# Attention queries projected between the second and third column group of the delta net's inputs, in both mixers

## The chip, the cores and the metric

The kernel runs on one core of a Trainium2 chip. The core has a matrix engine (PE), a vector engine (DVE), an activation engine (ACT), a general engine (POOL) and a queue that issues most transfers (SP). They run side by side, each takes its own instructions in a fixed order, and a semaphore holds an instruction until what it needs is done. The metric is device time of one execution in microseconds (us). The kernel before takes 3166.99 us (median of three runs, 3161.59 to 3169.63).

## The reference, cut to what matters

Two blocks follow each other on 256 tokens of width 1024, in float32. The first has two layers, and each layer begins with a mixer that feeds the same normalised input `h` to two branches: a differential attention (`da`) and a gated delta net (`dn`).

```python
proj = h @ w_in[l]
da_q, da_k, da_v, dn_q, dn_k, dn_v, dn_z, dn_b, dn_a, gates = jnp.split(proj, split_points, axis=-1)
y_a = diff_attention(da_q, da_k, da_v, ...)            # rms norm, rope, two softmaxes, difference
y_b = gated_deltanet(dn_q, dn_k, dn_v, dn_z, dn_b, dn_a, ...)
merged = g_a * (y_a @ w_branch_a[l]) + g_b * (y_b @ w_branch_b[l])
x = x + gt1 * (merged @ w_out[l])
h = rms_norm(x, norm2_g[l]) * (1.0 + sc2) + sh2
x = x + gt2 * (jnp.square(jax.nn.relu(h @ w_mlp1[l])) @ w_mlp2[l])
```

In `gated_deltanet`, q, k and v (512 columns each, columns 1536 to 3071 of `w_in`) pass a depthwise convolution over five tokens and a silu. Then q and k are normalised, and chunks of 64 tokens are put through a triangular solve, a scan in each direction, and a gated output norm. `da_q` is columns 0 to 511 of `w_in`, `da_k` and `da_v` the next two times 512. The second block (a sparse attention or a state space mixer, and a retrieval of experts) is computed by code that the change does not touch.

## The kernel before, in words

**Weights.** All large weights are loaded as tiles of 128x1024 floats in the order of one list, the plan, which `weights()` writes. A tile comes by a transfer into one of four raw buffers (`w_raw_t`). Then ACT rounds it to a reduced format (`w_hi`, line 238) and DVE subtracts to get the rest (`w_lo`, line 239). The pair goes into one of three pair buffers, so `w_hi` of a tile waits until PE is through with the tile three places earlier. The code asks for a pair two places ahead. Each product is taken as three matmuls (lines 318, 319, 320: high by high, high by low, low by high).

**Two forms of projection.** `proj_feat` puts out features on the partitions: 256 columns of weights are two tiles and 48 matmuls of 256 columns, and the result fills one PSUM bank. `proj_tok` puts out tokens on the partitions: 512 columns of weights are four tiles and 48 matmuls of 512 columns into two banks, one for each 128 tokens. PSUM banks come from three rings: psA has two banks, psB three, psC three.

**Start of a mixer (here called stage A).** The delta net's q, k and v are six column groups of 256, called cb0 to cb5. `dn(0)` is cb0 and cb1 (q), `dn(1)` is cb2 and cb3 (k), `dn(2)` is cb4 and cb5 (v). cb1 and cb3 go to psB, the others to psA. Each ends in `conv5`: ACT takes the middle tap (line 887), DVE adds four taps for each of two halves (line 891, eight instructions in all, which read the PSUM bank), ACT takes a tanh (893), DVE multiplies (894), PE transposes (line 324), ACT writes out (900). Then a small projection gives the delta net's gates (`exr`, lines 1430 and 1434: its result is copied by DVE, transposed by PE, and copied to `ba`).

**The woven part.** From there on, Python generators are interleaved by `weave`: decay and preparation of the delta net, the triangular solves (line 1249 is one of their matmuls), the scans (1321, 1328), the attention, and `project()`, which puts the remaining projections between them as work that PE can do while chains run on other engines. `project()` goes through `dn(2)`, then `tok` of da_q, da_k and da_v, then gates, z, gates. The attention's preparation of da_q and da_k squares on ACT (949), sums on DVE (950), normalises (957), and rotates with two halves on POOL (959, 960) and two instructions on DVE (961, 962). POOL also writes the masks `TT` of the solves (1208, 1209). Behind the weave `out` ends the delta net (lines 1358 to 1380), with the attention's branch projection (`ya`) beside it, and then follows the branch of the delta net (`yb`).

**What sets the order.** The program is written in this order, and the tile framework then sorts each engine's instructions with a simulated timeline of its own, so that one engine's order differs from the text within a stretch. Queues are in order on the chip.

Of the kernel before, what the change touches and what calls it, by code (L numbers as in the profile page):

```python
# [77 lines left out]
def weights(first=True):  # L78


    out, phase = [], 0

    def add(n, l, r0, c0, a, lane=None):
        out.append((phase, lane or f"m{phase}", n, l, r0, c0, a, 1024 // a))

    def tok(n, l, c0, rows=1024):
        for r0 in range(0, rows, 256):
            add(n, l, r0, c0, 2)

    def tok2(n, l, c0, lane=None):  # L90
        for r0 in (0, 512):
            add(n, l, r0, c0, 4, lane)

    def feat(n, l, c0, lane=None):
        for c in (c0, c0 + 128):
            add(n, l, 0, c, 8, lane)

    def mem_kv(l):
        feat("w_mem_kv_2", l, 0, "pm")
        tok2("w_mem_kv_2", l, 256, "pm")  # L100

    for l in range(2):
        for c0 in range(1536, 3072, 256):
            feat("w_in", l, c0)
        for c0 in (0, 512, 1024):
            tok("w_in", l, c0)
        for c0 in range(4624, 5648, 256):
            feat("w_in", l, c0)
        tok("w_in", l, 3072)
        for c0 in range(3600, 4624, 256):  # L110
            feat("w_in", l, c0)
        for j in (2, 3, 4) if l == 0 else (4,):
            for c0 in (1024 * j, 1024 * j + 512):
                for r0 in range(0, 1024, 256):
                    add("ada_w", l, r0, c0, 2, "plain")
        for n in ("w_branch_a", "w_branch_b"):
            for c0 in (0, 512):
                tok(n, l, c0, 512)
        for c0 in (0, 512):
            tok("w_out", l, c0)  # L120
        for g in range(17):
            if g < 16:
                feat("w_mlp1", l, 256 * g)
            if g == 9 and first:
                mem_kv(l)
            if g:
                for r0 in (256 * g - 256, 256 * g - 128):
                    add("w_mlp2", l, r0, 0, 1)
    if not first:
        out.clear()  # L130
        for l in range(2):
            mem_kv(l)
    for l in range(2):
        phase += 1
        if l == 0:
            n = "a_w_in_2"
            for c0 in (1024, 1280):
                feat(n, 0, c0)
            tok2(n, 0, 768)
            for c0 in (0, 256, 512, 1608):  # L140
                feat(n, 0, c0)
        else:
            n = "b_w_in_2"
            for c0 in (1536, 1792, 2060, 768, 1024, 1280):
                feat(n, 0, c0)
            tok(n, 0, 0)
            tok2(n, 0, 512)
        for c0 in (0, 512):
            tok("w_o_2", l, c0)
        for c0 in range(0, 2048, 256):  # L150
            feat("peer_w_q_2", l, c0)
        for i in range(128 + LAG):
            if i < 128:
                add("peer_u_2", l, 128 * i, 0, 1, f"u{l}" if i >= RAW else f"pu{l}")
            if i >= LAG:
                add("peer_v_2", l, 128 * (i - LAG), 0, 1, f"v{l}")
    return out
# [129 lines left out]
class K:  # L287
# [479 lines left out]
    def mixer1(self, c, Ls, l):  # L767
# [9 lines left out]
        done = set()  # L777
# [31 lines left out]
        def project():  # L809
            yield from dn(2)  # L810
            done.add("v")
            for i, n in enumerate(("daq", "dak", "dav")):
                yield from tok(dat[i])
                done.add(n)
                yield
# [8 lines left out]
            for _ in self.ada(L, (2, 3, 4) if l == 0 else (4,), self.st.plain):  # L824
                yield

        for i in range(2):
            for _ in dn(i):
                pass
        if l == 0:  # L830
            nc.sync.dma_start(self.ct, a["cst"][:, N1:N2])
        ba = sm.tile([128, 2, 16], F32, name="ba")
# [1434 lines left out]
```

## Time and profile before

| what | value |
|---|---|
| median of three runs | 3166.99 us |
| the profiled execution | 3168.19 us |
| its span in the trace | 3166.4 us |
| mean granted clock of PE | 0.96 |
| mixer of layer 0 in the trace | about 38 to 404 us |
| mixer of layer 1 in the trace | about 596 to 955 us |

The span is 1.8 us shorter than the execution's own time. PE is the engine with the most busy time (95%); its clock is either full or half, and 0.96 is a mean over both. In a timeline row the bracket gives how long the engine was idle just before the row and what it waited for. In a row of waits the three numbers are total time, times and the longest. In a row by form or line the last part is idle time before the group.

### The profile page before, as it was taken

Reading aid. Unit: us, or ns where it says so; the run is one execution under the profiler, and the core shown is the slowest. Engines: PE = TensorE matmul, PEld = TensorE weight load, DVE = VectorE, ACT = ScalarE, POOL = GpSimd, SP = SyncE. Lnnn points to the kernel's source line nnn. Section 1 sums busy time; section 2 is a strip of 40 time slices with the busy share of each in tenths; the row PEclk is TensorE's granted clock in tenths of the full one; section 3 lists DMA queues with packets and bytes.
Section 4 is the critical chain, followed back from the end, with each engine's and each line's share of the span. In section 5 each row is a group of like instructions: output and inputs, shape, how many; then the busy total and the mean of one; then the engine's idle time right before and its main releaser. Section 6 shows DMA issues by size and latency. Waiting matters only on the chain.

```text
span 3166.4 us, 54565 instructions
## 1 busy us (share of the span) xinstructions
PE 2994.7 (95%) x21010; PEld 2685.5 (85%) x21010; DVE 2464.6 (78%) x5317; ACT 1553.7 (49%) x2630; POOL 116.0 (4%) x95
## 2 busy tenths in 40 slices
PE   7999899899989999899999999997799999999998
PEld 6798799878869987888999999986588999999987
DVE  7888767886766568698878878777879887887877
ACT  5644455464545546425555455455433545554544
POOL 0211000011100001000000000000100000000000
PEclk9999899999989996899999999998799999999999
DMA  7425578533356651435555555453144555555544
GB/s 255 134 96 179 199 256 300 180 113 120 114 173 209 199 187 34 136 126 161 180 176 178 180 179 176 159 187 119 56 146 141 170 176 180 179 175 179 180 160 147
DMA packets 158201, 522.02 MB, mean 165 GB/s; under 512 B 17320, under 2 KB 24404, under 8 KB 157812
## 3 DMA queue, kind: packets, MB, share of 16 engines
q1 hardware_dynamic: 149408, 502.94, 47.9%
q10 hardware_dynamic: 7348, 11.39, 1.1%
q8 instruction: 165, 2.70, 0.4%
q0 software_dynamic: 1184, 4.19, 0.3%
q14 instruction: 96, 0.79, 0.1%
HBM read 514.23 MB, written 6.59 MB: 164 GB/s over the span
## 4 chain that ended last, share of the span: by engine, by line
PE 77%; DVE 13%; ACT 3%; DMA 3%; issue 2%; POOL 1%; SPq 0%; ACTq 0%; DVEq 0%; POOLq 0%
PE psA L318 14%; PE psA L320 13%; PE psA L319 13%; PE psB L318 8%; PE psB L320 8%; PE psB L319 8%; DVE w_lo L239 3%; PE psA L2013 2%; PE psB L2072 2%; PE psB L324 1%; ACT w_hi L238 1%; PE psB L1257 1%; DMA w_raw_t<-in_peer_u_dram 1%; PE psC L630 1%; PE psB L1249 1%
## 5 line engine op out<-in xcount | busy, mean ns | idle before, releaser
L238 ACT ACTIVATE w_hi<-w_raw_t 128x1024 fp32r<-128x1024 f32 x806 | 850.3, 1057 | 746.5 <-PE psB L319 372.7
L239 DVE TENSOR_TENSOR w_lo<-w_raw_t,w_hi 128x1024 fp32r<-128x1024 f32 x806 | 991.8, 1231 | 241.1 <-ACT w_hi L238 217.2
L318 PE MATMUL psB<-H,w_hi 128*128 128x256 f32 x2128 | 601.2, 283 | 2.8 <-ACT w_hi L238 2.8
L320 PE MATMUL psB<-H,w_lo 128*128 128x256 f32 x2128 | 601.3, 283 | 0.0
L319 PE MATMUL psB<-H,w_hi 128*128 128x256 f32 x2128 | 600.3, 282 | 0.0
L318 PEld LDWEIGHTS psB<-H,w_hi 128*128 128x128 f32 x2128 | 403.8, 190 | 12.2 <-ACT w_hi L238 3.4
L320 PEld LDWEIGHTS psB<-H,w_lo 128*128 128x128 f32 x2128 | 411.1, 193 | 0.6 <-DVE w_lo L239 0.3
L319 PEld LDWEIGHTS psB<-H,w_hi 128*128 128x128 f32 x2128 | 403.6, 190 | 8.4
L318 PE MATMUL psA<-w_hi,Wh 128*128 128x512 f32 x1024 | 390.8, 408 | 0.0
L319 PE MATMUL psA<-w_lo,Wh 128*128 128x512 f32 x1024 | 371.5, 389 | 0.0
L320 PE MATMUL psA<-w_hi,Wl 128*128 128x512 f32 x1024 | 370.4, 392 | 0.0
L318 PE MATMUL psA<-H,w_hi 128*128 128x256 f32 x1056 | 304.0, 289 | 13.0 <-DVE exy L1789 8.0
L320 PE MATMUL psA<-H,w_lo 128*128 128x256 f32 x1056 | 303.5, 288 | 2.8 <-DVE w_lo L239 2.6
L319 PE MATMUL psA<-H,w_hi 128*128 128x256 f32 x1056 | 301.9, 286 | 0.0
L2055 DVE TENSOR_TENSOR oj<-iop,pickj 128x1024 f16<-128x1024 f16 x256 | 176.4, 690 | 111.5 <-PE psB L2072 111.0
L327 ACT ACTIVATE Wh<-W 128x256 fp32r<-128x256 f32 x256 | 106.7, 419 | 316.4 <-issue 251.6
L320 PEld LDWEIGHTS psA<-w_hi,Wl 128*128 128x128 f32 x1024 | 191.8, 188 | 43.8
L319 PEld LDWEIGHTS psA<-w_lo,Wh 128*128 128x128 f32 x1024 | 193.1, 189 | 35.8 <-DVE w_lo L239 0.2
L318 PEld LDWEIGHTS psA<-w_hi,Wh 128*128 128x128 f32 x1024 | 192.3, 188 | 33.2
L318 PEld LDWEIGHTS psA<-H,w_hi 128*128 128x128 f32 x1056 | 204.3, 194 | 17.7 <-issue 10.7
L320 PEld LDWEIGHTS psA<-H,w_lo 128*128 128x128 f32 x1056 | 205.1, 194 | 4.8 <-DVE w_lo L239 4.0
L319 PEld LDWEIGHTS psA<-H,w_hi 128*128 128x128 f32 x1056 | 204.5, 194 | 1.0 <-issue 0.7
(593 smaller groups left out, 5012.1 us busy)
## 6 DMA issues: line engine op xcount, KB each, us to landing
w_raw_t<-in_wst_dram SPq DMA_DIRECT2D x368, 512.0 KB, 3.9
w_raw_t<-in_peer_u_dram SPq DMA_DIRECT2D x256, 512.0 KB, 3.3
w_raw_t<-in_peer_v_dram SPq DMA_DIRECT2D x256, 512.0 KB, 3.3
aw<-in_ada_w_dram SPq DMA_DIRECT2D x24, 1024.0 KB, 7.5
bd<-bd ACTq DMA_DIRECT2D x1, 2304.0 KB
H<-in_ada_w_dram SPq DMA_DIRECT2D x2, 1024.0 KB
gd<-ga ACTq DMA_DIRECT2D x4, 512.0 KB, 9.8
qkT<-gd ACTq DMA_DIRECT2D x4, 512.0 KB, 5.4
```

What stands on the lines that cost most here:

```text
L238: nc.scalar.activation(out=hi, in_=raw, func=AF.Copy)
L239: nc.vector.tensor_tensor(out=lo, in0=raw, in1=hi.bitcast(F32), op=OP.subtract)
L318: mm(ps, lhsT=lh, rhs=rh, start=first, stop=False)
L319: mm(ps, lhsT=lh, rhs=rl, start=False, stop=False)
L320: mm(ps, lhsT=ll, rhs=rh, start=False, stop=last)
L324: self.nc.tensor.transpose(out, in_, self.ident[:p, :p])
L327: self.nc.scalar.activation(out=hi, in_=src, func=AF.Copy, scale=scale)
L630: mm(ps[:, k:k + 1], lhsT=acc[:, k * 128:(k + 1) * 128], rhs=self.ones[:, 0:1], start=(i == 0), stop=(i == len(accs) - 1))
L1249: nc.tensor.matmul(px[:, hc(d, h)], lhsT=NT[d, t][:, hs(h)], rhs=cls(TI[d, t][:, hs(h)], s, 1 - d), start=True, stop=True)
L2013: nc.tensor.matmul(ps[:, 0:256], lhsT=w[:, k * 128:k * 128 + 128], rhs=whole[:, k, :], start=(k == 0), stop=(k == 7))
L2055: v.tensor_tensor(out=oj, in0=self.iop.unsqueeze(1).to_broadcast([128, H, 128, 2]), in1=two(pick[1][:, tb], 128), op=OP.is_equal)
L2072: nc.tensor.matmul(ps[:, 64 * k:64 * k + 64], lhsT=oj[:, x, :, y], rhs=oi[:, x, :, :, y].rearrange("p n i -> p (n i)"), start=True, stop=True)
```

## The change

The plan puts the tiles of `w_in` columns 0 to 511 (da_q, four tiles) behind the first two column groups of the delta net. Before, they stood behind all six. The code follows: after `dn(0)` it runs `tok(dat[0])` and then `dn(1)`, all in front of the weave, marks `daq` as done, and `project()` goes on from `dn(2)` with da_k. The instructions are the same in number and shape on every engine, apart from a few waits and register instructions. Line numbers grow by 3 from line 106 on and by 4 from about line 827 on.

```diff
--- before.py
+++ after.py
@@ -100,9 +100,12 @@
         tok2("w_mem_kv_2", l, 256, "pm")
 
     for l in range(2):
-        for c0 in range(1536, 3072, 256):
+        for c0 in (1536, 1792):
             feat("w_in", l, c0)
-        for c0 in (0, 512, 1024):
+        tok("w_in", l, 0)
+        for c0 in range(2048, 3072, 256):
+            feat("w_in", l, c0)
+        for c0 in (512, 1024):
             tok("w_in", l, c0)
         for c0 in range(4624, 5648, 256):
             feat("w_in", l, c0)
@@ -809,7 +812,7 @@
         def project():
             yield from dn(2)
             done.add("v")
-            for i, n in enumerate(("daq", "dak", "dav")):
+            for i, n in ((1, "dak"), (2, "dav")):
                 yield from tok(dat[i])
                 done.add(n)
                 yield
@@ -824,9 +827,10 @@
             for _ in self.ada(L, (2, 3, 4) if l == 0 else (4,), self.st.plain):
                 yield
 
-        for i in range(2):
-            for _ in dn(i):
+        for g in (dn(0), tok(dat[0]), dn(1)):
+            for _ in g:
                 pass
+        done.add("daq")
         if l == 0:
             nc.sync.dma_start(self.ct, a["cst"][:, N1:N2])
         ba = sm.tile([128, 2, 16], F32, name="ba")
```

Three places show how the orders differ. The names carry the buffer's number: `psA_529` is one allocation of a psA bank, `w_hi_476` and `w_lo_477` are one pair.

PE, mixer 0, behind the last matmuls of cb1 (psB_443). Before, cb2 stands there (psA_529):

```order
L318 MATMUL psB_443<-H0_241,w_hi_446 128x256
L319 MATMUL psB_443<-H1_242,w_hi_446 128x256
L320 MATMUL psB_443<-H0_241,w_lo_447 128x256
L318 MATMUL psA_529<-H0_241,w_hi_476 128x256
L319 MATMUL psA_529<-H1_242,w_hi_476 128x256
L320 MATMUL psA_529<-H0_241,w_lo_477 128x256
```

After, the da_q projection stands there. These are its rows at the step from the first 128 tokens (psA_529) to the second (psA_530, the bank that cb0's psA_345 had):

```order
L323 MATMUL psA_529<-w_hi_551,H1_242 128x512
L321 MATMUL psA_529<-w_hi_551,H0_241 128x512
L322 MATMUL psA_529<-w_lo_552,H0_241 128x512
L323 MATMUL psA_529<-w_hi_551,H1_242 128x512
L321 MATMUL psA_530<-w_hi_476,H0_241 128x512
L322 MATMUL psA_530<-w_lo_477,H0_241 128x512
L323 MATMUL psA_530<-w_hi_476,H1_242 128x512
L321 MATMUL psA_530<-w_hi_476,H0_241 128x512
```

Forty-eight matmuls of 512 columns have moved to this place, and the second bank of them is that of cb0.

DVE, at the same place: the convolution of cb0 (`exy_418`) and cb1 (`exy_504`). Before, these are the rows about the last instruction that reads cb0's bank:

```order
L239 TENSOR_TENSOR w_lo_649<-w_raw_t_530,w_hi_648 128x1024
L891 SCALAR_TENSOR_TENSOR exy_418<-psA_345,vec_93,exy_418 128x255
L891 SCALAR_TENSOR_TENSOR exy_590<-psA_529,vec_93,exy_590 128x254
L891 SCALAR_TENSOR_TENSOR exy_504<-psB_443,vec_93,exy_504 128x254
L891 SCALAR_TENSOR_TENSOR exy_418<-psA_345,vec_93,exy_418 128x254
L891 SCALAR_TENSOR_TENSOR exy_590<-psA_529,vec_93,exy_590 128x255
```

After, they are the rows from the third pair of da_q (`w_lo_552`) to that instruction:

```order
L242 TENSOR_TENSOR w_lo_552<-w_raw_t_444,w_hi_551 128x1024
L895 SCALAR_TENSOR_TENSOR exy_418<-psA_345,vec_93,exy_418 128x254
L895 SCALAR_TENSOR_TENSOR exy_504<-psB_443,vec_93,exy_504 128x254
L895 SCALAR_TENSOR_TENSOR exy_504<-psB_443,vec_93,exy_504 128x255
L895 SCALAR_TENSOR_TENSOR exy_418<-psA_345,vec_93,exy_418 128x254
L895 SCALAR_TENSOR_TENSOR exy_504<-psB_443,vec_93,exy_504 128x255
L895 SCALAR_TENSOR_TENSOR exy_418<-psA_345,vec_93,exy_418 128x255
L895 SCALAR_TENSOR_TENSOR exy_504<-psB_443,vec_93,exy_504 128x254
L895 SCALAR_TENSOR_TENSOR exy_418<-psA_345,vec_93,exy_418 128x255
L895 SCALAR_TENSOR_TENSOR exy_418<-psA_345,vec_93,exy_418 128x254
```

No convolution of a third group (`exy_590` before) stands among them any more, and nine convolution instructions are left between that pair and the release of cb0's bank.

DVE, mixer 0, about the last convolution instruction of cb2, whose bank cb5 takes next. Before, cb2 is psA_529 with `exy_590`, and `w_lo_1229` is the first pair of da_q, three places behind the second pair of cb4:

```order
L891 SCALAR_TENSOR_TENSOR exy_676<-psB_615,vec_93,exy_676 128x254
L891 SCALAR_TENSOR_TENSOR exy_590<-psA_529,vec_93,exy_590 128x255
L239 TENSOR_TENSOR w_lo_1229<-w_raw_t_915,w_hi_1228 128x1024
L891 SCALAR_TENSOR_TENSOR exy_1047<-psA_914,vec_93,exy_1047 128x254
L891 SCALAR_TENSOR_TENSOR exy_590<-psA_529,vec_93,exy_590 128x254
L891 SCALAR_TENSOR_TENSOR exy_676<-psB_615,vec_93,exy_676 128x254
```

After, cb2 is psA_605 with `exy_666`, cb4 is psA_1025, and `w_lo_1364` is the first pair of da_k, again three places behind cb4's second pair (`w_hi_1028`):

```order
L956 TENSOR_SCALAR ss_998<-ss_998 128x16
L895 SCALAR_TENSOR_TENSOR exy_666<-psA_605,vec_93,exy_666 128x255
L242 TENSOR_TENSOR w_lo_1364<-w_raw_t_1026,w_hi_1363 128x1024
L895 SCALAR_TENSOR_TENSOR exy_1170<-psA_1025,vec_93,exy_1170 128x254
L895 SCALAR_TENSOR_TENSOR exy_752<-psB_691,vec_93,exy_752 128x254
L341 TENSOR_SCALAR rs_i_1006<-ss_998 128x16
L895 SCALAR_TENSOR_TENSOR exy_666<-psA_605,vec_93,exy_666 128x254
```

The pair has kept its place in front of that last instruction, and small instructions of the da_q preparation (lines 956, 341) have come between.

PE, mixer 1, the end of `out`. Before, the last of its matmuls (line 1363) is followed by 43 matmuls of the attention's branch (`ya`):

```order
L1363 MATMUL psB_8802<-N11_7456,AT11_6776 64x128
L320 MATMUL psA_8979<-ya0_8191,w_lo_8910 128x256
L318 MATMUL psA_8979<-ya0_8191,w_hi_8969 128x256
L319 MATMUL psA_8979<-ya1_8192,w_hi_8969 128x256
L320 MATMUL psA_8979<-ya0_8191,w_lo_8970 128x256
L318 MATMUL psA_8979<-ya0_8191,w_hi_8969 128x256
```

After (line 1367), the transposes of `out` follow at once, and behind them the delta net's branch (`yb`):

```order
L1367 MATMUL psB_8802<-N11_7591,AT11_6899 64x128
L327 MATMUL psB_8859<-base_58,D1_8764 128x128 x4
L327 MATMUL psB_8894<-base_58,D1_8764 128x128 x4
L321 MATMUL psA_9053<-yb0_8829,w_hi_8975 128x256
L321 MATMUL psA_9084<-yb0_8829,w_hi_8975 128x256
L322 MATMUL psA_9053<-yb1_8830,w_hi_8975 128x256
L323 MATMUL psA_9053<-yb0_8829,w_lo_8976 128x256
```

The branch matmuls have moved ahead, in among the scan.

On POOL the rotation halves and the masks are in a new order. Before, in both mixers: masks `TT00`, `TT10`, `TT01`, then four halves of da_q, then `TT11`, then four of da_k. After, in mixer 1: two halves of da_q stand behind `TT00`, the other two between the two steps of `TT01`, two of da_k in front of `TT11`, and the last two between the two steps of `TT11`. In mixer 0 the first two of da_k stand between the two steps of `TT11` and the last two behind it.

## Rows read from the trace of the kernel before

**Rows 1.** The page, part 1: busy time by engine.

```profile
PE 2994.7 (95%) x21010; PEld 2685.5 (85%) x21010; DVE 2464.6 (78%) x5317; ACT 1553.7 (49%) x2630; POOL 116.0 (4%) x95
```

**Rows 2.** Timeline, PE, mixer 0, column groups 5 and 6 (start us, us, engine line operation).

```profile
69.64 0.28 PE L320 MATMUL psA<-H,w_lo 128*128 128x256 f32 x1
71.64 0.63 PE L324 MATMUL psC<-base,exy 128*128 128x128 f32 x4 [1.72 <-DVE exy L894]
74.33 0.35 PE L318 MATMUL psA<-H,w_hi 128*128 128x256 f32 x1 [2.07 <-DVE exy L891]
74.53 0.28 PE L319 MATMUL psA<-H,w_hi 128*128 128x256 f32 x1
74.64 0.28 PE L320 MATMUL psA<-H,w_lo 128*128 128x256 f32 x1
```

**Rows 3.** Windows of mixer 0 behind that wait (length, busy time and count by engine, clock).

```profile
75.20:78.60 3.40, 3.40 (x18) 3.40 (x17) 3.12 (x8) 1.08 (x2) 0.00 (x0) 0.50 0.27 105
78.60:82.00 3.40, 3.40 (x32) 3.40 (x31) 2.86 (x5) 3.15 (x13) 0.00 (x0) 1.00 0.00 0
```

**Rows 4.** Timeline, DVE, the same stretch.

```profile
72.19 1.21 DVE L239 TENSOR_TENSOR w_lo<-w_raw_t,w_hi 128x1024 fp32r<-128x1024 f32 x1
73.33 0.86 DVE L891 SCALAR_TENSOR_TENSOR exy<-psA,vec,exy 128x254 f32<-128x254 f32 x2
74.11 0.47 DVE L891 SCALAR_TENSOR_TENSOR exy<-psB,vec,exy 128x254 f32<-128x254 f32 x1
```

**Rows 5.** ACT by form, 36 to 92 us (count, busy, mean ns, idle before).

```profile
L238 ACT ACTIVATE w_hi<-w_raw_t 128x1024 fp32r<-128x1024 f32 x14 | 14.9, 1065 | 12.3 <-PE psA L319 8.1 <-ACT exy L887 1.6 <-issue 1.3
```

**Rows 6.** Timeline, PE, two matmuls of 512 columns.

```profile
99.34 0.39 PE L318 MATMUL psA<-w_hi,H 128*128 128x512 f32 x1
99.57 0.39 PE L319 MATMUL psA<-w_lo,H 128*128 128x512 f32 x1
```

**Rows 7.** Waits of PE in mixer 0, 36 to 340 us (total, times, longest).

```profile
PE psB L324 <- DVE ext L1430: 2.0, 1, 2.0
PE psC L324 <- DVE exy L894: 1.7, 1, 1.7
PE psC L324 <- DVE oo L1018: 1.1, 1, 1.1
```

**Rows 8.** Waits of PE in mixer 1, 596 to 960 us.

```profile
PE psB L324 <- DVE D L1380: 4.8, 1, 4.8
PE psC L324 <- DVE D L962: 2.7, 1, 2.7
PE psA L318 <- DVE exy L891: 2.1, 1, 2.1
PE psC L324 <- DVE exy L894: 1.5, 1, 1.5
```

**Rows 9.** Windows of mixer 0 (start:end, length, busy time and count by engine, clock).

```profile
36.00:92.00 56.00, 49.35 (x358) 46.03 (x359) 48.95 (x108) 33.15 (x76) 0.00 (x0) 0.97 0.49 160
168.00:257.00 89.00, 88.79 (x722) 83.66 (x721) 74.12 (x179) 44.97 (x98) 7.27 (x7) 1.00 0.38 126
257.00:298.00 41.00, 37.54 (x278) 34.60 (x277) 31.81 (x79) 16.40 (x42) 7.98 (x7) 0.88 0.34 110
```

**Rows 10.** Windows of mixer 1 about the wait for L962.

```profile
727.10:737.40 10.30, 10.30 (x49) 10.30 (x50) 4.88 (x7) 1.35 (x3) 0.00 (x0) 0.50 0.16 52
737.40:745.00 7.60, 7.60 (x55) 6.08 (x54) 2.16 (x7) 2.77 (x7) 0.00 (x0) 1.00 0.00 0
```

**Rows 11.** Lines by form, 640 to 730 us: POOL's rope.

```profile
L960 POOL TENSOR_TENSOR exr<-D,ropes 128x256 f32<-128x256 f32 x4 | 5.8, 1449 | 0.0
L959 POOL TENSOR_TENSOR exr<-D,ropes 128x256 f32<-128x256 f32 x4 | 3.7, 924 | 4.1 <-DVE exy L894 2.4 <-DVE D L962 1.8
```

**Rows 12.** Windows of mixer 1, the end of the delta net.

```profile
878.30:883.50 5.20, 5.20 (x45) 5.19 (x45) 4.45 (x18) 1.23 (x2) 0.00 (x0) 1.00 0.01 2
883.50:888.90 5.40, 0.58 (x6) 0.35 (x5) 4.97 (x14) 1.89 (x3) 0.00 (x0) 0.88 0.38 107
```

## The prediction

> **What bounds the kernel now.** I began with the page's busy times: PE is busy for 95% of the span and DVE for 78% [rows 1]. So the order of PE's work can gain only where PE waits, or where its clock is low. The list of PE's waits in the two mixers came next, since the change moves nothing outside them: it shows a few waits of 1 to 5 us, nearly all of them for DVE [rows 7, 8]. The windows tell where PE is the bound. In the solves of mixer 0 PE is busy for 88.79 of 89.00 us. In stage A it is busy for 49.35 of 56.00 with DVE at 48.95, so the two share that stage. Behind the last solve it is busy for 37.54 of 41.00, at a mean clock of 0.88 [rows 9]. Last came timelines and windows about the waits of stage A [rows 2 to 4].
>
> In stage A, cb4's last matmul starts at 69.64 and cb5's first at 74.33. Between them stand waits of 1.72 and 2.07 us with four transposes [rows 2]. Behind DVE's `w_lo`, which starts at 72.19, come three convolution instructions, and the second one at 73.33 frees cb5's bank [rows 4]. That pair is three places behind cb4's second pair, so its `w_hi` could not start before PE had done with cb4. The wait thus belongs to the ring of three pairs more than to DVE's load.
>
> **The change part by part.** The counts of instructions stay as they are, so the sum of this change is what PE's idle time and low clock become. One projection is 48 matmuls at 0.23 us, 99.34 to 99.57 [rows 6], so 11.0 us of PE work comes into stage A and leaves later stages. Counted in the two orders, it leaves as follows. Mixer 0: 2.1 us before the first solve, 6.1 in the solves, 2.8 behind them. Mixer 1: nothing before the first solve, 3.4 in the solves, 1.8 from there through the scan, 5.9 from the first of `out`'s matmuls on. A matmul of 256 columns counts 0.11 us there, 74.53 to 74.64 [rows 2]. Where the work leaves a stretch in which PE never waits, the stretch gets that much shorter and the move costs nothing. Six points remain.
>
> *The new bank step.* The second bank of da_q is cb0's, and DVE must finish cb0's convolution first. From cb1's last matmul on: `w_hi_551` takes 1.06 us [rows 5], since its buffer is the one of cb1's second pair. Its `w_lo` takes 1.14 from start to start, and nine convolution instructions take 0.39 each (two in 0.78, 73.33 to 74.11) [rows 4]. That is 1.06 + 1.14 + 9 x 0.39 = 5.7 us, against 18 x 0.23 = 4.1 us of matmuls into the first bank. The new wait is 1.6 us, up to 2.0 with the semaphores; I take 1.8 in each mixer, 3.6 in both. If DVE has a backlog there it is more, and if ACT prepares early, less: 0 to 3.
>
> *The old bank step (cb4 to cb5).* The chain stays: w_hi 1.06, w_lo 1.14, then three convolution instructions and a small one, 1.4, together 3.6 us. The two waits before are 1.72 + 2.07 = 3.8 us in mixer 0 [rows 2], and 2.1 + 1.5 = 3.6 in mixer 1 [rows 8]. I count nothing. If DVE stands 0.5 us behind, it is +0.5; if the extra 11 us had let DVE catch up, the wait would go (first rival).
>
> *The clock.* After the wait of 2.07 us the granted clock is 0.50 for 3.4 us, the lower level, and then 1.00 again [rows 3]. That costs half of it, 1.7 us. A new wait may bring such a stretch. I count none, and 1.7 us in each mixer at the high end.
>
> The Trainium skill, page "TensorE: Matmul & The Clock Gate", section "A second HAM failure mode: psum-queue depth-cycling", says that short idle times between groups of matmuls that cycle through PSUM banks can make the clock swing between its two levels, and that the loss is in throughput. The rows agree that it can follow such a wait. By that rule the sum below would be 3.4 us higher.
>
> *The rope and the masks.* In mixer 1 PE waits 2.70 us for da_q's or da_k's rotation (962) [rows 8], and the clock then stays at 0.50 for 10.30 us [rows 10], which costs half of it, 5.15 us. Together that is 7.85. With da_q ready some 50 us earlier, half of POOL's rotations stand earlier, and DVE has lost the da_q preparation there. But two rotation halves now stand between the steps of the last mask, 0.92 + 1.45 = 2.4 us of POOL [rows 11], and the last solve's start waits for it. The ends are -7.9 and +2.4. I take -3.9: the wait shrinks but part of the low clock stays.
>
> *Behind the solves in mixer 0.* 2.8 us of cover leaves a stretch where PE already waits on chains (1.1 for `oo`) [rows 7], and where it is idle for 3.5 of 41 us [rows 9]. Ends 0 and +2.8; I take the middle, +1.4.
>
> *`out` in mixer 1.* Before, 43 branch matmuls fill 878.3 to 883.5, and then PE waits 4.8 us for the chain through DVE's 1380 [rows 8, 12]. DVE is busy for 4.45 of those 5.20 us and for 4.97 of the next 5.40 [rows 12], so the chain is DVE's. With the branch matmuls gone ahead, the chain stays and PE idles for 10 us instead of 4.8. So 5.2 us of the moved work saves nothing. DVE has up to two fewer branch instructions in the way, some 0.8 us. I take +4.4; ends +2 (DVE's chain was longer for the branch) and +6 (the clock stays low for longer).
>
> The sum: 3.6 + 0 + 0 - 3.9 + 1.4 + 4.4 = +5.5 us. On the profiled execution of 3168.19 us (span 3166.4 and 1.8 around it) that is 3173.7. The median stands 1.2 below that execution, so I forecast 3172.5.
>
> **The rivals.**
>
> *The inserted work is cover.* Between cb1 and cb2 DVE gets 11 us in which PE has other work, and could clear all its convolutions. Then both waits of stage A vanish: 3.8 us and 1.7 of low clock in mixer 0, 3.6 and 1.7 in mixer 1, 10.8 in all. With the rope's -7.9 and the +5.8 of the late stages the time is 3166.99 - 12.9 = 3154. For it: two `w_lo` fewer wait in a burst. Against it: the pair chain behind cb4 is the same as before in the new order.
>
> The Trainium skill, page "Perfetto Trace Analysis", section "Matmuls", asks that independent groups rotate through PSUM banks so that the evacuation of one overlaps the matmuls of the next. By that rule this rival's gain is the one to expect. The trace shows two banks in rotation and a wait in spite of it.
>
> *PE work is interchangeable.* If PE is the bound wherever work leaves, if the new wait takes the place of part of the old, and if the rope and `out` terms cancel, nothing changes: 3167. The 95% speak for it; `out` speaks against it.
>
> *Uncovered chains (slower).* One mechanism: filler that hid the chains of the solve's end, the scan and `out` is spent early, and PE waits there. The price is all that leaves behind the solves (2.8 + 7.7), with the 3.6 of the new wait, 3.4 of low clock and the mask's +2.4: 3166.99 + 19.9 = 3187. It decides where a stretch has less than about 3 us of filler for each round. The solves keep theirs; the last stretches do not.
>
> **How the numbers follow.** My forecast has 0.48, with a range of its own of 3165 to 3181. Cover has 0.25, interchangeable 0.12, uncovered chains 0.15. About 0.3% (9.5 us, 3157.5 to 3176.5) is what a measurement of this kernel can tell from no change. Of the cover case three quarters fall below 3157.5, with a little of the forecast: 0.21 faster. Nearly all of the uncovered case and a fifth of the forecast lie above 3176.5: 0.24 slower. The same: 0.55. The range that leaves out a tenth at each end is 3156 to 3187.
>
> **What would show it.** Right: in the profile after, da_q's matmuls in stage A with a wait of 1.6 to 2.0 us for 895 in their middle; again 3 to 4.5 us of waits in front of cb5; the first gate transposes (for `ext`) 12.5 to 14 us later in the mixer than before; a PE wait of about 10 us for line 1384 in mixer 1; the wait for 966 shorter. Wrong: no wait in front of cb5; no long wait at `out`; a wait for 1213 over 4 us at the last mask, or the first solve starting later by more than the work that moved ahead of it.

## The result: 0.5% slower, and the first mixer holds all of it

| kernel | median, us | runs | ratio to before (95%) |
|---|---|---|---|
| before | 3166.99 (3159.24 to 3169.63) | 7 | |
| changed | 3181.03 (3175.86 to 3188.21) | 7 | 1.0053 (1.0042 to 1.0065) |

The medians stand 14.0 us apart. The profiled execution of the changed kernel took 3184.92 us, a span of 3183.1.

The page after, part 1, has the same busy time for DVE and a little more for PE than [rows 1], in a span that is 16.7 us longer:

```profile
PE 3001.2 (94%) x21010; PEld 2686.1 (84%) x21010; DVE 2464.9 (77%) x5317; ACT 1554.1 (49%) x2630; POOL 116.8 (4%) x95
```

The waits of PE in mixer 0 after (36 to 340 us; total, times, longest), which answer to [rows 7]:

```profile
PE psA L321 <- ACT w_hi L241: 4.7, 2, 4.0
PE psC L633 <- DVE acc L655: 4.5, 1, 4.5
PE psA L321 <- ACT exy L891: 3.9, 1, 3.9
...
PE psB L327 <- DVE ext L1434: 2.0, 1, 2.0
PE psA L321 <- DVE exy L895: 2.0, 1, 2.0
PE psB L1166 <- DVE TT L1169: 1.8, 1, 1.8
```

The 2.0 for line 895 is the new wait in the middle of da_q. The 3.9 for line 891 stands in front of cb5, in the place of the two waits of [rows 2]. (In the changed kernel 891 is ACT's middle tap, which was 887. The last DVE instructions that read cb2's bank, line 895, start at 88.71 us.) The first two rows (4.0 us of the first) stand at the end of the mixer and were in no term of mine. The next rows are PE's timeline after (start, us, instruction, idle before), and then windows (start:end, length, busy time and count of each engine, clock) behind these waits:

```profile
56.59 0.39 PE L323 MATMUL psA<-w_hi,H 128*128 128x512 f32 x1
58.94 0.47 PE L321 MATMUL psA<-w_hi,H 128*128 128x512 f32 x1 [1.96 <-DVE exy L895]
...
89.34 0.36 PE L321 MATMUL psA<-H,w_hi 128*128 128x256 f32 x1 [3.85 <-ACT exy L891]
```

```profile
58.90:62.30 3.40, 3.36 (x10) 2.73 (x11) 2.21 (x5) 2.94 (x3) 0.00 (x0) 0.67 0.00 1
62.30:65.70 3.40, 3.40 (x16) 2.73 (x16) 2.97 (x4) 2.46 (x3) 0.00 (x0) 0.83 0.36 118
89.30:92.80 3.50, 3.46 (x22) 3.50 (x23) 3.50 (x12) 1.09 (x2) 0.00 (x0) 0.71 0.33 122
```

The new wait is 1.96 us, and in this trace a stretch of low clock follows: 3.4 x 0.33 + 3.4 x 0.17 = 1.7 us. The wait in front of cb5, 3.85, has its own, as the one before had [rows 3].

Mixer 1 after, which answers to [rows 8] (596 to 960 us):

```profile
PE psB L327 <- DVE D L1384: 5.8, 2, 3.2
...
PE psA L321 <- ACT exy L891: 3.9, 1, 3.9
PE psB L327 <- DVE ext L1434: 2.4, 1, 2.4
PE psA L321 <- DVE exy L895: 2.0, 1, 2.0
...
PE psC L327 <- DVE D L966: 1.0, 2, 0.5
```

Stage A has the same two waits. The wait for the rotation (966) is 1.0 instead of 2.7. The wait at `out` (1384) is 5.8 in two pieces, where I had expected about 10. These are PE's rows there, before and then after:

```profile
877.78 0.44 PE L1363 MATMUL psB<-N,AT 128*64 128x128 f32 x4
888.92 1.17 PE L324 MATMUL psB<-base,D 128*128 128x128 f32 x4 [4.84 <-DVE D L1380]
```

```profile
899.60 0.44 PE L1367 MATMUL psB<-N,AT 128*64 128x128 f32 x4
902.80 1.17 PE L327 MATMUL psB<-base,D 128*128 128x128 f32 x4 [2.60 <-DVE D L1384]
907.19 1.17 PE L327 MATMUL psB<-base,D 128*128 128x128 f32 x4 [3.22 <-DVE D L1384]
```

**Where the time went, by stretch.** I cut each mixer at five marks that both kernels have: cb0's first matmul, the gate transposes (for `ext`), the first and the last matmul of line 1249 (1253), and the first matmul of the delta net's branch (`yb`). Stage A lies before the gate transposes; "to solve" runs from there to the first solve. The windows of mixer 0, before and then after:

```profile
38.70:91.90 53.20, 46.86 (x346) 43.93 (x346) 46.15 (x104) 30.59 (x72) 0.00 (x0) 0.97 0.47 151
91.90:168.30 76.40, 71.77 (x436) 61.62 (x437) 66.92 (x162) 53.15 (x83) 25.24 (x16) 0.96 0.43 140
168.30:258.30 90.00, 89.79 (x732) 84.66 (x730) 75.08 (x184) 45.76 (x99) 7.27 (x7) 1.00 0.37 124
258.30:332.10 73.80, 65.23 (x492) 59.14 (x491) 59.91 (x144) 24.84 (x51) 7.98 (x7) 0.86 0.46 155
```

```profile
38.70:107.00 68.30, 59.78 (x394) 54.17 (x394) 54.99 (x124) 37.39 (x80) 0.00 (x0) 0.95 0.45 149
107.00:185.60 78.60, 70.25 (x434) 60.04 (x435) 65.66 (x152) 50.98 (x81) 27.20 (x19) 0.98 0.39 133
185.60:268.20 82.60, 81.76 (x698) 78.36 (x697) 64.11 (x160) 36.51 (x82) 5.20 (x5) 1.00 0.29 102
268.20:346.20 78.00, 65.71 (x478) 58.06 (x478) 62.35 (x157) 28.82 (x63) 8.20 (x7) 0.85 0.46 158
```

Stage A is 15.1 us longer for 11.0 us of work. The solves are 7.4 shorter for 6.1 of work: PE is busy there for 89.79 of 90.00 us, and what leaves is saved. The stretch to the first solve is 2.2 longer though 2.1 of work left it, and PE idles 8.35 us in it instead of 4.63. The stretch behind the last solve is 4.2 longer though 2.8 left it, and PE idles 12.3 instead of 8.6. In this mixer the two stretches that wait on other engines gave nothing back.

One execution each is little to go by. Two of the kernels below run a mixer 0 with the same order of instructions: "mixer 1 changed" has the one of before, "mixer 0 changed" the changed one. Their windows for the stretch to the first solve and the stretch behind the last one, in that order of kernels:

```profile
91.10:169.00 77.90, 70.79 (x435) 60.67 (x436) 67.03 (x162) 53.26 (x83) 25.25 (x16) 0.98 0.41 137
259.00:336.30 77.30, 70.16 (x492) 62.38 (x492) 59.95 (x143) 24.94 (x51) 7.84 (x7) 0.82 0.43 147
```

```profile
107.10:185.70 78.60, 71.27 (x434) 61.08 (x435) 65.78 (x152) 50.97 (x81) 27.18 (x19) 0.96 0.39 133
268.20:345.80 77.60, 62.80 (x479) 55.75 (x479) 62.12 (x157) 28.93 (x63) 8.22 (x7) 0.89 0.45 159
```

Behind the last solve PE's idle time grew in both: 12.3 and 14.8 us against 8.6 and 7.1. To the first solve it is 8.4 and 7.3 against 4.6 and 7.1, so there the growth is not clear of chance.

Lengths by stretch, from the starts of the marks in all the traces (us):

| kernel | mixer 0: A, to solve, solves, behind | whole | mixer 1: A, to solve, solves, behind | whole |
|---|---|---|---|---|
| before | 53.2, 76.3, 90.0, 73.8 | 337.7 | 51.5, 71.9, 95.5, 74.7 | 339.1 |
| mixer 1 changed | 52.4, 77.9, 90.0, 77.3 | 340.0 | 65.4, 71.3, 85.4, 71.8 | 339.2 |
| changed | 68.3, 78.6, 82.5, 78.0 | 349.9 | 67.3, 72.3, 85.4, 73.7 | 344.5 |
| mixer 0 changed | 68.5, 78.6, 82.5, 77.5 | 349.5 | 50.6, 70.6, 91.0, 76.3 | 334.2 |
| da_q on psB | 72.9, 79.1, 81.3, 78.5 | 357.1 | 69.8, 75.5, 83.3, 62.6 | 336.5 |
| before, cb5 on psB | 52.4, 67.2, 82.0, 117.3 | 361.2 | 51.8, 67.2, 83.2, 92.5 | 337.0 |
| before, accumulators | 53.1, 77.9, 90.0, 74.8 | 341.4 | 51.6, 72.0, 91.0, 77.8 | 337.6 |
| changed, accumulators | 68.7, 78.6, 83.6, 80.5 | 353.8 | 67.4, 72.5, 85.2, 65.4 | 335.4 |
| changed, both edits | 71.9, 78.8, 81.3, 82.7 | 361.3 | 69.4, 75.4, 85.6, 60.7 | 338.0 |
| before, short columns | 54.5, 76.3, 86.8, 73.8 | 336.3 | 51.6, 72.0, 91.1, 76.6 | 336.8 |
| changed, short columns | 67.2, 80.2, 82.4, 75.2 | 351.0 | 65.7, 72.3, 85.3, 65.3 | 333.2 |
| da_q third | 58.9, 80.5, 81.0, 84.3 | 348.8 | 56.4, 77.0, 87.5, 75.7 | 341.8 |
| before, thin da_q | 52.6, 90.0, 82.7, 84.3 | 356.4 | 50.0, 74.8, 88.6, 73.2 | 332.2 |
| changed, thin da_q | 71.2, 80.9, 81.3, 77.7 | 356.4 | 64.1, 78.6, 92.6, 77.0 | 358.4 |

"Whole" runs on to the first transpose of the next norm. Each row is one execution. Rows with the same order of instructions (mixer 0 of the first two, mixer 0 of the next two) differ by 2.3 us as a whole and by up to 3.5 in one stretch, so that much is chance in one execution.

### The profile page after: what moved, and what is told of

Read it like the earlier page. It is cut to its first block, busy times and chain, and to the rows that moved or that the text cites. A ratio compares the mean times of both kernels' runs of the same rounds, so it can differ in the third digit from the quotient of the medians.

```text
span 3183.1 us, 54593 instructions
## 1 busy us (share of the span) xinstructions
PE 3001.2 (94%) x21010; PEld 2686.1 (84%) x21010; DVE 2464.9 (77%) x5317; ACT 1554.1 (49%) x2630; POOL 116.8 (4%) x95
## 4 chain that ended last, share of the span: by engine, by line
PE 75%; DVE 14%; ACT 4%; DMA 3%; issue 2%; POOL 1%; ACTq 0%; SPq 0%; DVEq 0%; POOLq 0%
PE psA L321 14%; PE psA L323 14%; PE psA L322 13%; PE psB L321 8%; PE psB L323 8%; PE psB L322 8%; DVE w_lo L242 2%; PE psB L2076 2%; PE psB L327 1%; ACT w_hi L241 1%; DMA w_raw_t<-in_wst_dram 1%; PE psB L1253 1%; PE psB L1261 1%; PE psC L633 1%; PE psB L1267 1%
## 6 DMA issues: line engine op xcount, KB each, us to landing
H<-in_ada_w_dram SPq DMA_DIRECT2D x2, 1024.0 KB, 12.8
```

## The experiments

Each kernel was timed in five rounds beside the kernel before. The ratios are to that kernel in the same job.

**One mixer at a time.** The edit makes the plan, the order of the calls and `project()` depend on the layer (this is the first run; the second has `l == 1`):

```diff
-        for g in (dn(0), tok(dat[0]), dn(1)):
+        for g in (dn(0), tok(dat[0]), dn(1)) if l == 0 else (dn(0), dn(1)):
```

> The change in the first layer's mixer alone; the second layer's mixer is as before. Theory (three terms, each at its own place: new bank wait with a half-clock stretch in stage A, adaLN columns that stand later on DVE, no relief from the rope): the trace of the changed kernel has the first mixer end 12.0 us later, so +12 us (9 to 14) against the kernel before. Rival (the loss is a general one of less filler, the same in both mixers): +7 us, half of the 14 measured.

Measured: 1.0046 (1.0032 to 1.0060), some 15 us (10 to 19). The rival's +7 is outside, the theory's +12 inside; of the theory's three places, the adaLN columns fell later (below).

> The change in the second layer's mixer alone. Theory: stage A +4.8, solves with the rope -6.8, out +6.7, together +4.7 us less 1.6 behind it: +3 us (1 to 6), and with the first mixer's result the sum is that of the whole change, 14 us. Rival (same in both mixers): +7 us.

Measured: 0.9992 (0.9977 to 1.0006). The theory's +3 is only just outside the interval, the rival's +7 far out. Within their intervals the two results add up to the whole change, and the first mixer makes all of it. In the table its mean is 349.7 where changed against 338.8, +10.9 us. Over the four kernels each that are as before or as changed in mixer 1, that mixer has 336.9 and 338.1, +1.2. The four changed ones fall into two pairs, though: behind the last solve they have 73.7 and 71.8 us, or 65.4 and 65.3. PE's order and its idle time there are nearly the same (7.7 to 8.0 us); the clock is not. These are the windows of the changed kernel and of "changed, short columns":

```profile
835.40:909.05 73.65, 65.92 (x449) 54.98 (x448) 44.08 (x114) 25.96 (x55) 7.95 (x7) 0.84 0.12 44
833.70:899.00 65.30, 57.59 (x448) 48.40 (x447) 43.70 (x114) 26.20 (x55) 7.95 (x7) 0.96 0.14 49
```

So a term of a few us behind mixer 1's last solve cannot be read from one trace.

**da_q's second bank from another ring.** This takes away the wait for cb0's bank (`tok` hands the banks on):

```diff
-        for g in (dn(0), tok(dat[0]), dn(1)):
+        for g in (dn(0), tok(dat[0], lambda: [self.psA(), self.psB()]), dn(1)):
```

> The changed kernel, with the second bank of the early da_q projection taken from the psB ring, so that it does not wait for cb0's convolution. Theory (the bank is what PE waits for, and the half clock follows from that wait): the waits of 1.96 and 2.03 us in the middle of da_q go, the matmuls behind them run at 0.23 instead of 0.32 us, and the gate transposes come 3.6 us earlier in each mixer; -5 to -8 us against the changed kernel, +6 to +9 against the one before. Rival (DVE has the same backlog, the wait moves to cb5): the wait in front of cb5 grows from 3.85 to 5.5 to 7 us, the gate transposes stay within 1 us of 107.0, and the time stays at +14.

Measured: 1.0051 (1.0038 to 1.0064), no gain. PE's timeline of this kernel:

```profile
64.45 0.39 PE L323 MATMUL psB<-w_hi,H 128*128 128x512 f32 x1
64.68 0.28 PE L321 MATMUL psA<-H,w_hi 128*128 128x256 f32 x1
...
94.41 1.11 PE L327 MATMUL psC<-base,exy 128*128 128x128 f32 x4 [6.40 <-DVE exy L898]
```

cb2 starts at 64.68 instead of 68.28 us, so the 3.6 us were won at that place: the bank was what PE waited for, and from 57 to 68 us the clock is 1.00. Then PE waits 6.40 us for DVE's 898, at transposes, where it had waited 3.85 in front of cb5. The gate transposes came at 111.65, outside the rival's 1 us, with 30 more matmuls of da_k in front of them (some 6.9 us). The rival was right about the wait that moves and about the time. That DVE's convolutions set the pace of stage A fits this, but the order changed with the edit, so it is argued and not shown.

**The kernel before with cb5 on another ring.** The same idea for the two waits of [rows 2]:

```diff
-                                                self.psB() if cb in (1, 3) else None)
+                                                self.psB() if cb in (1, 3, 5) else None)
```

> The kernel before, with cb5's bank taken from the psB ring, so that cb5 does not wait for cb2's convolution. Theory (bank is the binding wait, cb5's pair is ready): the waits of 2.07 and 2.12 us for line 891 go, with most of the half clock behind them, cb5 begins at about 71 instead of 74.3 us; the gate transposes come 2 to 5 us earlier, since DVE is busy for 46 of 53 us there and cannot follow the whole way; -3 to -8 us in all. Rival (the pair ring or DVE binds, the wait moves on to da_q or to the copy of ext): the gate transposes move by less than 1 us and the time by less than 2 us.

Measured: 1.0102 (1.0085 to 1.0119), 32 us slower. The wait for 891 moved to da_q, and the gate transposes moved by 0.8 us, so the rival was right on stage A. The rest I had not foreseen. The last solve of mixer 0 is 18 us earlier, and the delta net's branch begins 25 us later. Windows of mixer 0 behind the last solve of this kernel:

```profile
240.30:300.00 59.70, 59.70 (x437) 53.47 (x435) 48.13 (x104) 34.80 (x71) 11.23 (x7) 1.00 0.47 160
300.00:345.00 45.00, 24.19 (x175) 19.48 (x174) 38.59 (x101) 6.36 (x9) 0.00 (x0) 0.68 0.64 224
```

PE is full up to 300 us, and then half idle for 45 us at a clock of 0.68. The solves got ahead of the projections, and what was left for the end is chains with nothing beside them.

**More accumulators for the adaLN columns.** In the changed kernel the third of six column groups starts at 296.5 us on DVE, 28 behind the last solve (before: 274.3, 16 behind). It needs an accumulator that PE frees by its sums (633), and these stand behind the attention's last transposes. Four more accumulators in the dead buffer H0 take that wait away:

```diff
-                acc = self.adp.tile([128, 512], F32, tag="acc", name="acc", bufs=2)
+                if take == self.st.plain and ring == 2:
+                    spare = self.ar.get("H0", 2048)
+                acc = self.adp.tile([128, 512], F32, tag="acc", name="acc", bufs=2) if take != self.st.plain or \
+                    ring < 2 else spare[:, 512 * ring - 1024:512 * ring - 512]
+                ring += 1
```

> The changed kernel, with four more accumulators for the adaLN column groups of the first mixer (in the buffer of the normalised input, which is dead by then), so that the third group does not wait until PE has summed the first. Theory (the end of the first mixer is set by these columns: the third group starts at 296.5 us, 28 behind the last solve, because PE's sums stand behind the attention's last transposes): the third group starts some 20 to 25 us earlier, PE's waits of 4.50 us (for the accumulator) and 3.96 us (for the first branch weights) go, the delta net's branch begins at 334 to 340 instead of 346.2; -6 to -12 us against the changed kernel, so +2 to +8 against the one before. Rival (DVE and the transfers need that time in any case): the branch begins less than 3 us earlier, and the time stays at +11 to +15.

Measured: 1.0051 (1.0038 to 1.0064). DVE's timeline (the group's first instruction) in the changed kernel, and with the edit:

```profile
296.48 0.47 DVE L650 TENSOR_SCALAR acc<-w_raw_t,cT 128x512 f32<-128x512 f32 x1
```

```profile
273.02 0.49 DVE L654 TENSOR_SCALAR H<-w_raw_t,cT 128x512 f32<-128x512 f32 x1
```

PE's waits behind the last solve with the edit (265 to 352 us):

```profile
PE psC L327 <- DVE mod L672: 3.3, 1, 3.3
PE psC L327 <- DVE oo L1026: 2.3, 1, 2.3
PE psB L1329 <- DVE yb L1343: 2.2, 2, 1.6
PE psB L1295 <- DVE TI L1250: 2.2, 1, 2.2
```

The group starts 23 us earlier, and the waits of 4.50 and 3.96 us are gone. Others of 2 to 3 us stand there now, for the columns' result (672), the attention (1026), the scan (1343) and the solves' merge (1250), and PE idles 12.1 us in that stretch, as before the edit (12.3). The branch begins at 350.2 instead of 346.2 us. So the wait for the accumulator was real, but taking it away won nothing: this theory fell.

> The kernel before with the same four accumulators. Theory: its third group already starts at 274.3, 16 us behind the last solve, so there is less to win: it starts 5 to 10 us earlier, the branch of the delta net at 326 to 331 instead of 332.1, -1 to -6 us. Rival (nothing but transfer and DVE time): within 1 us of the kernel before.

Measured: 1.0005 (0.9993 to 1.0017), as the rival has it.

> The changed kernel with both edits: da_q's second bank from psB, and the four accumulators. The first edit took the wait of 1.96 us and its half clock out of stage A, but the first mixer ended later. Theory (its gain of 2 to 4 us was lost behind the solves to the columns, whose third group stood at 294.8): with the accumulators the gain comes through; -2 to -5 us against the changed kernel with the accumulators alone, 0 to +5 against the one before. Rival (the bank edit loses by its order of the solves, its last solve is at 272.0 instead of 268.1): no better than the accumulators alone, +2 to +10.

Measured: 1.0045 (1.0029 to 1.0061). No better than the accumulators alone, and mixer 0 is the longest of all (361.3 us).

**A quarter of the columns' work.** If DVE's load behind the solves were the cause, taking most of it away would close the gap:

```diff
-                    for r0 in range(0, 1024, 256):
+                    for r0 in (range(0, 1024, 256) if l else (0,)):
...
-                while k0 < 8:
+                kn = 2 if l == 0 and take == self.st.plain else 8
+                while k0 < kn:
```

> The kernel before with a quarter of the adaLN columns' work in the first mixer: of the eight row blocks of each of its six column groups only the first two are loaded and summed (6 weight tiles instead of 24), so the gates and shifts of that layer are computed from part of the sum. Both theories: faster than the kernel before, by 3 to 25 us, as 18 tiles with 36 DVE instructions of 0.7 us leave. It is the partner of the next run.

Measured: 1.0021 (1.0005 to 1.0037). Not faster at all, though DVE had 36 instructions fewer: both theories were wrong on this.

> The changed kernel with the same quarter of the columns' work in the first mixer. Theory (the work that left the solves' end uncovers chains there because DVE is full with these columns, so their DVE work decides): the difference to the kernel before with the same cut shrinks from 14 us to between -3 and +5, as in the second mixer, which has a third of the columns and loses nothing. Rival (the loss is made before the last solve, in stage A and in front of the first solve, where PE's idle time grew by 2.1 and 3.7 us and the clock fell): the difference stays at +8 to +15.

Measured: 1.0049 (1.0028 to 1.0070), 9.4 us by the medians above its partner. That lies at the rival's lower edge. By the two intervals the difference can be anything from about 1 to 17 us, so the times alone leave the theory's +5 open. In the traces mixer 0 is 351.0 against 336.3 us, 14.7 longer, and that speaks for the rival: with most of the columns' work cut the loss is still there. Stage A (67.2 against 54.5) and the stretch to the first solve (80.2 against 76.3) lose 16.5 together, and the solves give back 4.4.

**da_q behind all of q and k.** The plan follows the calls:

```diff
-        for g in (dn(0), tok(dat[0]), dn(1)):
+        for g in (dn(0), dn(1), tok(dat[0])):
```

> da_q still ahead of the weave in both mixers, but behind all of q and k (column groups 1 to 4) instead of between groups 2 and 3. The work that leaves the woven part is the same. Theory (what counts is that 11 us of filler leave the woven part; the place in stage A decides only the 3 to 4 us of the bank wait with its half clock): +8 to +14 us against the kernel before. Rival (the place between groups 2 and 3, with the wait for cb0's bank, makes the loss): within 5 us of the kernel before.

Measured: 1.0079 (1.0062 to 1.0097), some 25 us: slower than the change, and above the theory's range as well as the rival's. The place between groups 2 and 3 does not make the loss. The gate transposes come at 98.2 us, only 6.3 later than before for 11.0 us of work, since waits of 2.5 and 1.3 us are all that is left in stage A. Yet mixer 0 ends up 11 us longer: the first solve starts 10.4 us late, and the stretch behind the last one is 10.5 longer. What stage A won is lost further on.

**Less PE work.** The first of da_q's three products alone, in the kernel before and in the changed one:

```diff
+                if thin:
+                    self.nc.tensor.matmul(ps[t][:, 0:m], lhsT=hT[0][:, kk, s], rhs=w.hi[:, j, :],
+                                          start=kk == 0, stop=kk == kt - 1)
+                    continue
```

> The kernel before with a third of da_q's matmuls: only the product of the two high parts is taken (16 matmuls instead of 48 in each mixer), so da_q is less exact; all else is done as before. 32 x 0.23 = 7.4 us of PE work leave each mixer, 2.8 in stage A and 4.6 in the woven part. Theory (from the gate transposes to the first solve, and from the last solve to the delta net's branch, a chain on other engines sets the time, so PE work that leaves there saves nothing; only the solves and part of stage A are PE's): -1 to -7 us in all, with the stretch from the gate transposes to the first solve within 2 us of 76.3 in the first mixer. Rival (PE work is interchangeable and PE is the bound): -12 to -15 us.

Measured: 1.0031 (1.0016 to 1.0045), slower with 14.8 us less PE work in both mixers together. PE's waits from the gate transposes to the first solve of mixer 0:

```profile
PE psA L319 <- DVE w_lo L239: 4.8, 1, 4.8
PE psA L476 <- DVE spna L1399: 2.4, 1, 2.4
PE psA L476 <- ACT w_hi L238: 1.9, 1, 1.9
```

That stretch grew from 76.3 to 90.0 us, with PE's idle time at 12.4 instead of 4.6 and a mean clock of 0.87 instead of 0.96. So it is not PE's work that sets its length; but both sums failed, and the theory's "within 2 us" as well. The waits of 2.4 and 1.9 are of da_q's own matmuls (476), the second for their weights. The longest (4.8) is of a later projection, 7 us in front of the first solve. The order is another one, too.

> The changed kernel with the same third of da_q's matmuls; all 7.4 us leave stage A in each mixer. Theory (what stands in stage A is paid there, less what the wait for cb0's bank takes back, 2.7 us, as the first bank's matmuls are over sooner): -4 to -6 us in each mixer, -8 to -12 in all against the changed kernel, so +2 to +6 against the one before, and the gate transposes at 102 to 104 us instead of 107.0. Rival (DVE sets stage A, so that less PE work there saves nothing): gate transposes at 106 to 108, and +10 to +14.

Measured: 1.0097 (1.0077 to 1.0116). The row at the new bank step, and the window behind it:

```profile
60.03 1.19 PE L479 MATMUL psA<-w_hi,H 128*128 128x512 f32 x2 [4.38 <-DVE exy L899]
```

```profile
60.00:63.40 3.40, 3.37 (x9) 2.49 (x10) 2.20 (x5) 3.39 (x4) 0.00 (x0) 0.50 0.00 0
```

The bank comes free at 60.0 us, no earlier than in the changed kernel (58.9), so PE waits 4.38 instead of 1.96, and cb2 starts at 67.58 against 68.28: of 7.4 us saved in work 0.7 arrive. The gate transposes came at 110.2. The rival was right that less PE work saves nothing in stage A, though it too had the transposes too early and the sum too low. Mixer 1 of this kernel is 358.4 us, 14 longer than in the changed kernel, and no run tells why.

## Why the prediction held, and what was wrong in it

The kernel became slower by 14.0 us (0.44% by the medians, 0.53% by the ratio), inside the range of 3156 to 3187. The likeliest case had +5.5 and "the same". 3181.03 is at the very end of that case's own range, and the case with the chance of 0.24 came about. So it was the width of the range (31 us) that held. The sum was 8.5 us low, and in the traces most of that is mixer 0: its terms give +3.2 (1.8 and 1.4), and it became 10.9 longer. Compared with the sum, stage A took 2.8 more (15.6 longer for 11.0 + 1.8), the stretches to the first solve and behind the last 3.6 each, and the solves and the rest 2.3 less.

*The signs.* The waits at the new bank step and in front of cb5 came, and the wait for 966 was shorter. The gate transposes were later than 12.5 to 14 us, and the wait at 1384 is 5.8 in two pieces instead of about 10. One sign of being wrong came too: the first solve of mixer 0 starts 17.3 us later in the mixer, for 11.0 us of work ahead of it.

*The new bank step* was right: 1.6 to 2.0 us forecast, 1.96 and 2.03 measured (mixer 1's row stands at 628.92 with 2.03).

*The old bank step* was right: again 3 to 4.5 us was forecast, and 3.85 in mixer 0 and 3.9 in mixer 1 came. The chain of cb4, the pair ring and the convolution is as it was, so the first rival's cover was not to be had. The rule of the Trainium skill (page "Perfetto Trace Analysis", section "Matmuls") that groups should rotate through banks, by which that cover was to be expected, does not decide here: with a bank more the wait moved on to the next user (3.85 became 6.40 us).

*The clock* was counted at nothing. In stage A of mixer 0 the low clock amounts to 3.4 us in both changed traces and to 1.7 in both of before (length times the missing share of the clock), so +1.7. It does not hang on the new wait alone. In the kernel with mixer 0 changed, which has the same order there, the wait is as long, and no low clock follows:

```profile
59.97 0.47 PE L323 MATMUL psA<-w_hi,H 128*128 128x512 f32 x1 [2.03 <-DVE exy L898]
```

```profile
60.00:63.40 3.40, 3.40 (x15) 2.81 (x16) 2.20 (x6) 2.76 (x3) 0.00 (x0) 1.00 0.02 5
```

There the whole 3.4 us stand about the wait in front of cb5 (87 to 93 us). The rule of the Trainium skill (page "TensorE: Matmul & The Clock Gate", section "A second HAM failure mode: psum-queue depth-cycling") tells of a kernel in which short idle times between groups of matmuls make the clock swing. The rows agree in part, since one of the two traces shows it at the new wait, and the sum by that rule, 3.4 us higher, was the better one. The gate transposes are 15.1 us late, where 12.5 to 14 was forecast; the low clock is most of the rest.

*The rope and the masks* (-3.9) came out near its size, for a reason that I had only in part. The wait of 2.70 us was a chance event: three other kernels whose second mixer is written as before show no such wait. Windows of the solves of mixer 1, in the kernel before, with mixer 0 changed, and in the changed kernel:

```profile
720.60:816.10 95.50, 92.80 (x702) 86.65 (x700) 60.39 (x144) 42.05 (x91) 7.69 (x7) 0.95 0.36 117
```

```profile
731.60:822.60 91.00, 91.00 (x702) 84.93 (x700) 60.69 (x145) 42.27 (x91) 7.68 (x7) 0.96 0.37 125
```

```profile
750.00:835.40 85.40, 84.36 (x708) 79.80 (x706) 66.64 (x162) 42.35 (x94) 3.69 (x3) 1.00 0.48 158
```

The same work takes 91.0 us in three of four traces, without a gap. The 2.70 us of [rows 8] were no property of the order. The low clock was: it stands in all four traces of before (0.95 or 0.96) and in none of the four with mixer 1 changed (1.00). All four of before have a wait of 1.8 us for POOL's last mask (1209), and in the three without the 2.70 us the low clock begins about 1 us behind it. In the changed ones POOL's new order leaves 0.4 us of waits for the masks (1213). So the change did bring relief there: the solves are 6.8 us shorter in the mean (85.3 against 92.1) with 3.4 of work gone, 5.7 shorter without the trace that has the wait. The price of +2.4 at the last mask did not come. That the mask wait starts the low clock is argued from its place.

*`out` in mixer 1* (+4.4) was mis-sized. PE does wait at once behind the last matmul of `out`, but from its start to that of the last transpose 8.1 us pass (899.77 to 907.89) instead of 11.7: with the branch's instructions out of DVE's way the chain is 3.6 us shorter, where I had allowed 0.8. Over four kernels each, the stretch behind the last solve is 7.3 us shorter in mixer 1 (69.0 against 76.4), nearly all of the 7.7 that left. The two traces without a further edit are only 2.8 shorter (72.7 against 75.5), with the low clock shown above. PE's idle time fell in all four, from between 9.2 and 9.5 us to between 7.7 and 8.0, so no chain lost its cover. That mixer 1's terms (+2.3) come near its +1.2 is luck: `out` was 4 too high, and stage A, 15.1 longer for 12.8 in the sum, was too low.

*Behind the solves in mixer 0* (+1.4) and *to the first solve* (nothing) are the steps that failed. The stretch behind grew by 2.2 us in the mean of two traces each (77.8 against 75.5), and 2.8 had left it: a loss of 5.0, with PE's idle time up in both. The stretch to the first solve grew by 1.5 (78.6 against 77.1), and 2.1 had left it: 3.6. The growth itself is no larger than the spread of the two traces of before (76.3 and 77.9); what is shown is that the 2.1 did not come back. I had let work leave that stretch for free since PE is 94% busy in it. It is busy, and still not what sets the time. Both changed traces have a wait of 1.8 us there for the decay's TT (1169), which neither trace of before has; no run takes it away.

So the third rival's mechanism, chains without cover, is what the end of mixer 0 shows. Its price had 7.7 us for mixer 1 as well, and there it did not happen. Where it would not happen could not be told from the filler per stretch, and no trace gives the 3 us for each round that the rival names.

What stays open: which chain sets the stretches of mixer 0. Taking away the wait for the accumulators, most of the columns' DVE work, or the place between groups 2 and 3 did not give the loss back. This speaks against each of them, but does not rule them out, since the order of several engines at once changes with each edit. Every reordering that was run made mixer 0 longer (341 to 361 us) than the two orders closest to before (336 to 340). No run is shown to be faster than the kernel before.

## What to carry to other kernels

Work put in front of the part that it used to cover cost its full length there, and more (15 us for 11.0). In mixer 0 it came back only from the stretch where PE waits for nothing; "94% busy" did not make a stretch one of these. In mixer 1 it came back at the end as well, although PE waits there, so the list of waits alone did not tell. Look, too, at how far a wait or a stretch of low clock recurs in other executions or layers before a term is built on it. And where a scheduler orders the engines, one edit moves chains far away: the waits in the trace of before tell what is removed, and only the next trace what comes instead.

## What was not expected of the hardware

Taking 14.8 us of PE work out made both kernels slower, by 0.3% and, against the changed kernel, by another 0.4%. In the traces PE's idle time grew by 14.5 us (before) and 21.2 us (changed), and its busy time did not fall (2994.6 against 2994.7 us, 3005.0 against 3001.2), since more of it ran at low clock (mean 0.953 against 0.960, 0.951 against 0.958); one such stretch, at 0.50, stands behind the longer wait (60.0 to 63.4 us above). And 18 weight tiles of 512 KB with their 36 DVE instructions, taken out of mixer 0, saved nothing that could be measured.
